# Making the low part of some weight chunks by an accumulating transfer in a hybrid attention layer

## The chip, the cores and the metric

One Trainium2 chip, one of its cores. The metric is device time in microseconds for one execution of the whole layer, as the median of several runs. TensorE is written PE, VectorE DVE, ScalarE ACT, GpSimd POOL, and SyncE, from which most transfers are issued, SP.

## What is computed

One decoder layer on 1024 tokens of width 2048: RMSNorm, one input projection, two groups of heads (a chunked gated delta rule and a chunked causal spatial gate), then one output projection with residual and a final RMSNorm. Only its end matters here:

```python
mix = jnp.concatenate([o_a, o_b], axis=-1) @ w_out[l].astype(x.dtype)
h = h + mix
...
return rms_norm(h, final_norm_w)
```

`w_out` is 2048 x 2048, all in float32.

## The kernel before

Every float32 product is made of three matmuls of a reduced format (float32r). Each operand is split into a high part, the value rounded, and a low part, what the rounding left; the product is high*high + high*low + low*high. `split` (L133) does this: a cast on ACT writes the high part (L135), a subtract on DVE writes the low part from the raw value and the high part (L136).

The output phase (`out_phase`, L850) is a Strassen-like scheme. Left operand and `w_out` are cut into 2 x 2 blocks, and `PRODUCTS` (L809) lists seven block products; for each it names the block or sum of two blocks of the left side, the same of `w_out`, and the blocks of the result to which it is added. In products 0, 2 and 6 (`SUMS`) the sum of two `w_out` blocks has been put into DRAM earlier (`wc_d`); in products 3 and 4 (`SUMB`) it is added on the fly (`wb`, L188); products 1 and 5 use one block as it lies in `w_out`.

Each product runs over two column halves `cb`, and in each over eight chunks k of 128 rows. One chunk is a 128 x 512 piece of the weights, 256 KB: 12 matmuls of 512 columns (L981 high*high, L982 with the low part of the weights, L983 with the low part of the left side) for four row tiles `t`. That is 7 x 2 x 8 = 112 chunks. `prep` (L892) gets a chunk ready: `w_chunk` (L183) loads it into a raw tile `wro` from SP's queue and splits it into `who` and `wlo`; in half 0 `a_prep` does the same for the left operand (`ar`, summed at L885, split into `a`). `run` (L214) prepares chunks three ahead of the one being multiplied. Raw tiles have three buffers (tag `wr`), high and low parts four each (tags `wh`, `wl`), so the cast of a chunk can start only when the fourth chunk before it has been multiplied.

After the last chunk of a half, `evac` (L909) adds the four accumulated tiles into the result blocks `c` on DVE (L919), for a block's first time together with the residual `xres`, loaded through two buffers. `finish` (L925) squares a block that is complete on ACT (`sqh`, L931) and multiplies it by the final norm's weights on POOL (L933), or, for the last quarter of a row tile, computes the row's scale in eleven small steps on DVE (`sth`), scales the four quarters (L951 on DVE, L955 on ACT) and writes them out (L956).

The order on each engine is that of the program after a scheduling layer has placed each instruction; every engine then runs its own list strictly in order. Product 5 is the one in whose first half the rows finished by product 4 are scaled and written out.

Of the kernel before, what the change touches and what calls it, by code (L numbers as in the profile page):

```python
# [8 lines left out]
F32 = mybir.dt.float32  # L9
F32R = mybir.dt.float32r  # L10
I32 = mybir.dt.int32
AF = mybir.ActivationFunctionType
ALU = mybir.AluOpType
# [4 lines left out]
P = 128  # L18
DM = 2048
SEQ = 1024  # L20
T = 512
# [10 lines left out]
def kernel(ctx, tc, x_tok, x_t, w_in, w_v0, w_vb, w_out, conv_w, norm_w, a_log, dt_bias,  # L32
                       hn_w, sgu_w, sgu_b, wsp_t, b_sp, fn_w, out):
    nc = tc.nc
# [98 lines left out]
    def split(hi, lo, src):  # L133

        nc.scalar.copy(hi, src)  # L135
        nc.vector.tensor_tensor(lo, src, hi.bitcast(F32), op=ALU.subtract)  # L136
# [43 lines left out]
        nc.scalar.copy(rb, rp)  # L180
        return rb

    def w_chunk(src, shape, name, keep=None, raw=None, add=None):  # L183
        if raw is None:
            raw = wp.tile(shape, F32, tag="wr", bufs=3, name=f"wr{name}")
        nc.sync.dma_start(raw, src)
        if add:
            nc.vector.tensor_tensor(raw, raw, add[0], op=add[1])  # L188
        hi, lo = keep or (wp.tile(shape, F32R, tag="wh", name=f"wh{name}"), wp.tile(shape, F32R, tag="wl", name=f"wl{name}"))
        split(hi, lo, raw)  # L190
        return hi, lo


# [38 lines left out]
    def w_tile(hf, ct, q):  # L232
        return w_chunk(w_in[ct, :, q * KH:(q + 1) * KH, :], [P, KH, P], f"{hf}_{ct}_{q}")
# [29 lines left out]
    def first_tiles(hf, xs, env, done):  # L263
# [3 lines left out]
        for q in range(KT // 2):  # L267
            def prep(q=q):
                ks = slice(2 * q, 2 * q + 2)
                raw = wp.tile([P, 2, 2, P], F32, tag="wr", bufs=3, name=f"wrf{hf}_{q}")  # L270
                hi = wp.tile([P, 2, 2, P], F32R, tag="wh", name=f"whf{hf}_{q}")
                lo = wp.tile([P, 2, 2, P], F32R, tag="wl", name=f"wlf{hf}_{q}")
                sqs_, sqs[:] = list(sqs), []
                for i in range(2):
                    x, sq = x_load(hf, 2 * q + i)
                    xs.append(x)
                    sqs.append(sq)
                    nc.sync.dma_start(raw[:, i], w_in[(H, 0)[i], :, ks, :])
                    split(hi[:, i], lo[:, i], raw[:, i])
                if q % 3 == 0:  # L280
                    vraw.append(big.tile([P, 3, 2, 288], F32, tag="b8", name=f"v0r{hf}_{q}"))
                v2 = big.tile([P, 2, 2, 288], F32R, tag="b8", name=f"v0{hf}_{q}")[:, :, :, 0:V0]
                vb = w_chunk(w_v0[q], None, None, (v2[:, 0], v2[:, 1]), vraw[-1][:, q % 3, :, 0:V0])
                for sq in sqs_ + (sqs if q == KT // 2 - 1 else []):
                    sq()
                if hf == 0 and q == 5:
                    conv_constants()
                return hi, lo, vb
# [480 lines left out]
    def group_b(hf, xs, st):  # L769
# [3 lines left out]
        for blk in range(1, 4):  # L773
            for k2 in range(KT // 2):
                def mm(w, blk=blk, k2=k2):
                    hi, lo = w
                    if blk == 1 and k2 == 0:
                        sb["rb"] = st["rb"]
                        env["vn"] = st["vn"] + [big.tile([P, NT, T], F32, tag="b8", name=f"vn{hf}_1")]
                    if k2 == 0:  # L780
                        env["acc"] = [proj_bank(f"vb{hf}_{blk}_{i}").rearrange("p (t c) -> p t c", c=256) for i in range(2)]
                    acc, vn = env["acc"], env["vn"]
                    for k in (2 * k2, 2 * k2 + 1):
                        xh, xl = xs[k]
                        for t in range(NT):
                            a, tsl = acc[t // 2][:, t % 2, :], slice(t * P, (t + 1) * P)
                            first, last = k == 0 and t % 2 == 0, k == KT - 1
                            for l, r, fl, sp_ in ((xh, hi, first, False), (xh, lo, False, False), (xl, hi, False, last)):
                                nc.tensor.matmul(a, l[:, tsl], r[:, k % 2, :], start=fl, stop=sp_, skip_group_check=True)  # L789
                        if k % 2 == 0:  # L790
                            tick()
                    if k2 == KT // 2 - 1:
                        for t in range(NT):
                            v = vsl(vn, t, blk * 256, (blk + 1) * 256)
                            nc.scalar.copy(v, acc[t // 2][:, t % 2, :])
                            nc.vector.bn_stats(st["st"][:, t, blk, :], v)
                        if blk == 3:
                            spawn(task_ln(hf, vn, st["st"], sb))
                    tick()
                yield (lambda blk=blk, k2=k2: w_chunk(w_vb[blk - 1, k2], [P, 2, 256], f"vb{hf}_{blk}_{k2}")), mm  # L800
# [26 lines left out]
    def w_quarter(b, cb, k):  # L827

        return w_out[b[1] * 2 + cb, b[0] * HK + k]
# [20 lines left out]
    def out_phase():  # L850
# [29 lines left out]
        def a_prep(n, k):  # L880
            spec = PRODUCTS[n][0]
            src = a_raw(n, spec[0], k)
            if len(spec) > 1:
                dst = src if spec[0] not in KEPT else wk.tile([P, T], F32, tag="cv", bufs=3, name=f"as{n}_{k}")
                nc.vector.tensor_tensor(dst, src, a_raw(n, spec[1], k), op=op[spec[2]])  # L885
                src = dst
            hi, lo = (wk.tile([P, T], F32R, tag=tag, bufs=bufs, name=f"a{i}{n}_{k}")
                      for i, (tag, bufs) in enumerate(ASLOTS[2 * k:2 * k + 2]))
            split(hi, lo, src)
            return hi, lo  # L890

        def prep(n, cb, k):  # L892
            src = w_quarter(PRODUCTS[n][1][0], cb, k) if n not in SUMS else \
                wc_d[SUMS.index(n), cb, k].rearrange("p (o c) -> p o c", o=1)
            keep = None
            if n == LAST and cb == 1 and k < HK - 4:
                keep = [act.tile([P, 1, T], F32R, tag="ah", name=f"wk{i}_{k}") for i in range(2)]
            add = None
            if n in SUMB:
                tag, bufs = SUMB[n]  # L900
                add = wk.tile([P, 1, T], F32, tag=tag, bufs=bufs, name=f"wb{n}_{cb}_{k}")
                nc.sync.dma_start(add, w_quarter(PRODUCTS[n][1][1], cb, k))
                add = add, op[PRODUCTS[n][1][2]]
            w = w_chunk(src, [P, 1, T], f"o{n}_{cb}_{k}", keep, add=add)
            if cb == 0:
                return w, a_prep(n, k)
            return w, None
# [88 lines left out]
        for n in range(LAST + 1):  # L996
            for cb in range(2):
                for k in range(HK):
                    if n == LAST and cb == 1:
                        yield (lambda k=k: prep(LAST, 1, k)), (lambda w, k=k: first_mm(w, k))  # L1000
                    else:
                        yield (lambda n=n, cb=cb, k=k: prep(n, cb, k)), \
                            (lambda w, n=n, cb=cb, k=k: mm(w, n, cb, k, range(NT)))
# [57 lines left out]
```

## Time and profile before

| | us |
|---|---|
| median of 3 runs | 1775.75 |
| lowest and highest | 1774.19, 1779.86 |
| the profiled execution, its own time | 1777.34 |
| its span, first to last instruction | 1775.6 |
| PE busy | 1729.8 (97%) |
| DVE busy | 1265.6 (71%) |
| ACT busy | 736.2 (41%) |
| POOL busy | 261.6 (15%) |
| mean granted TensorE clock | 0.993 |

The profile page gives busy time by engine, the chain of work that ended last, and the costliest groups of instructions by line. A timeline row has start and duration in us, engine, line, output and inputs by the program's names, and in brackets how long the engine had been idle before and who released it. Where an engine waits is read from those brackets; a matmul of 512 columns takes 0.39 us from start to end, but the next one starts 0.23 us after it, since they overlap.

### The profile page before, as it was taken

The numbers are of one execution on the slowest core, as the hardware profiler recorded it, in microseconds if no ns is written. First come the engines' busy times: TensorE is split into PE (matmuls) and PEld (weight loads), VectorE is DVE, ScalarE is ACT, GpSimd is POOL, SyncE is SP. The second block draws the span as 40 slices with busy tenths as digits, with TensorE's granted clock in tenths as the row PEclk, the third lists the DMA queues.
The fourth block names the chain that finished last, engine by engine and source line by source line (L and its number), as shares of the span: only waits on it lengthen the run. The fifth ranks groups of instructions, "written<-read, shape, count | busy, mean of one in ns | idle before, by whom it ended". The sixth has DMA issues, their size and how long they took to land.

```text
span 1775.6 us, 27440 instructions
## 1 busy us (share of the span) xinstructions
PE 1729.8 (97%) x9334; PEld 1456.9 (82%) x9334; DVE 1265.6 (71%) x2985; ACT 736.2 (41%) x1670; POOL 261.6 (15%) x314
## 2 busy tenths in 40 slices
PE   9999999999999999999999999999989999999997
PEld 8778888888997788887887778889878888878876
DVE  7798797987747533758979789794764346777885
ACT  7543534445333222646344443533422233333463
POOL 4120131211201200203012112120030000200121
PEclk9999999999999999999999999999999999999999
DMA  7455445364548734426543535544784457656774
GB/s 240 126 132 139 112 118 151 95 173 133 146 141 259 221 105 127 124 68 172 129 132 89 163 105 151 133 132 116 225 259 115 115 185 235 195 167 188 219 234 148
DMA packets 188893, 275.88 MB, mean 155 GB/s; under 512 B 37936, under 2 KB 70736, under 8 KB 188496
## 3 DMA queue, kind: packets, MB, share of 16 engines
q1 hardware_dynamic: 184064, 261.50, 50.8%
q0 software_dynamic: 4544, 12.62, 2.8%
q8 instruction: 73, 1.20, 0.3%
q14 instruction: 68, 0.56, 0.1%
q10 hardware_dynamic: 144, 0.01, 0.0%
HBM read 224.73 MB, written 49.32 MB: 154 GB/s over the span
## 4 chain that ended last, share of the span: by engine, by line
PE 64%; DVE 16%; DMA 11%; issue 4%; ACT 3%; POOL 1%; SPq 1%; DVEq 0%; ACTq 0%; POOLq 0%
PE acc L239 12%; PE acc L242 12%; PE acc L240 12%; PE vb L789 7%; PE oa L983 3%; PE oa L982 3%; PE oa L981 3%; DVE wl L136 2%; DVE cv L414 2%; DMA ar<-mix_d 2%; DMA xres<-x_tok 2%; DMA ws<-w_out 2%; PE ds L633 1%; PE p L622 1%; DVE fst L567 1%
## 5 line engine op out<-in xcount | busy, mean ns | idle before, releaser
L239 PE MATMUL acc<-xh,wh 128*128 128x512 f32 x1472 | 591.8, 402 | 1.0 <-ACT wh L135 1.0
L242 PE MATMUL acc<-xh,wl 128*128 128x512 f32 x1472 | 577.6, 392 | 5.1 <-DVE wl L136 5.0
L240 PE MATMUL acc<-xl,wh 128*128 128x512 f32 x1472 | 577.1, 392 | 0.0
L135 ACT CAST wh<-wr 128x512 fp32r<-128x512 f32 x368 | 226.1, 618 | 447.2 <-PE acc L240 310.8
L136 DVE TENSOR_TENSOR wl<-wr,wh 128x512 fp32r<-128x512 f32 x368 | 256.7, 700 | 144.2 <-ACT wh L135 139.2
L242 PEld LDWEIGHTS acc<-xh,wl 128*128 128x128 f32 x1472 | 277.6, 189 | 64.9 <-DVE wl L136 6.6
L239 PEld LDWEIGHTS acc<-xh,wh 128*128 128x128 f32 x1472 | 278.1, 189 | 58.0 <-issue 3.0
L240 PEld LDWEIGHTS acc<-xl,wh 128*128 128x128 f32 x1472 | 278.4, 189 | 51.7
L982 PE MATMUL oa<-wlo,a 128*128 128x512 f32 x432 | 168.4, 390 | 2.3 <-DVE wlo L136 2.3
L981 PE MATMUL oa<-who,a 128*128 128x512 f32 x432 | 168.3, 390 | 0.9 <-DVE pczb L405 0.5
L983 PE MATMUL oa<-who,a 128*128 128x512 f32 x432 | 168.2, 389 | 0.7 <-DVE a L136 0.7
L414 DVE SCALAR_TENSOR_TENSOR cv<-pc,cw,cv 128x511 f32<-128x511 f32 (+1 forms) x144 | 110.9, 770 | 8.7 <-ACT cv L411 7.2
L789 PE MATMUL vb<-whvb,xh 128*128 128x256 f32 x384 | 110.5, 288 | 0.0
L789 PE MATMUL vb<-wlvb,xh 128*128 128x256 f32 x384 | 108.6, 283 | 0.0
L789 PE MATMUL vb<-whvb,xl 128*128 128x256 f32 x384 | 108.6, 283 | 0.0
L135 ACT CAST who<-wro 128x512 fp32r<-128x512 f32 x108 | 66.5, 618 | 86.4 <-PE oa L983 41.0
L982 PEld LDWEIGHTS oa<-wlo,a 128*128 128x128 f32 x432 | 81.1, 188 | 20.3 <-DVE wlo L136 3.5
L136 DVE TENSOR_TENSOR wlo<-wro,who 128x512 fp32r<-128x512 f32 x108 | 77.9, 726 | 27.0 <-ACT who L135 26.7
L981 PEld LDWEIGHTS oa<-who,a 128*128 128x128 f32 x432 | 81.1, 188 | 18.4 <-DVE pczb L405 1.0
L983 PEld LDWEIGHTS oa<-who,a 128*128 128x128 f32 x432 | 81.1, 188 | 17.9 <-DVE a L136 1.2
L567 DVE TENSOR_TENSOR fst<-fs 32x31 f32<-32x31 f32 (+15 forms) x248 | 90.4, 365 | 4.2
L569 DVE TENSOR_TENSOR fs<-fs,fst 32x31 f32<-32x31 f32 (+15 forms) x248 | 87.3, 352 | 3.9
(248 smaller groups left out, 2482.1 us busy)
## 6 DMA issues: line engine op xcount, KB each, us to landing
wr<-w_in SPq DMA_DIRECT2D x368, 256.0 KB, 3.3
ws<-w_out SPq DMA_DIRECT2D x64, 256.0 KB, 4.1
wro<-w_out SPq DMA_DIRECT2D x64, 256.0 KB, 3.1
wrvb<-w_vb SPq DMA_DIRECT2D x48, 256.0 KB, 2.7
wc_d<-ws SPq DMA_DIRECT2D x48, 256.0 KB, 3.2
ar<-mix_d SPq DMA_DIRECT2D x48, 256.0 KB, 3.8
wro<-wc_d SPq DMA_DIRECT2D x48, 256.0 KB, 2.7
xr<-x_t SPq DMA_DIRECT2D x32, 256.0 KB, 3.8
```

What stands on the lines that cost most here:

```text
L135: nc.scalar.copy(hi, src)
L136: nc.vector.tensor_tensor(lo, src, hi.bitcast(F32), op=ALU.subtract)
L239: nc.tensor.matmul(acc, hi[:, kk, :], xh, start=(k == 0), stop=False)
L240: nc.tensor.matmul(acc, hi[:, kk, :], xl, start=False, stop=(last and lo is None))
L242: nc.tensor.matmul(acc, lo[:, kk, :], xh, start=False, stop=last)
L414: nc.vector.scalar_tensor_tensor(cv[:, s:], acc[:, :T - s], w, cv[:, s:], op0=ALU.mult, op1=ALU.add)
L567: nc.vector.tensor_tensor(tv, bc(lu[:, k, k + 1:].unsqueeze(2), [32, n, m]), bc(xu[:, k:k + 1, 0:m], [32, n, m]), op=ALU.mult)
L569: nc.vector.tensor_tensor(xu[:, k + 1:, 0:m], xu[:, k + 1:, 0:m], tv, op=ALU.subtract)
L789: nc.tensor.matmul(a, l[:, tsl], r[:, k % 2, :], start=fl, stop=sp_, skip_group_check=True)
L981: nc.tensor.matmul(acc[t], ah[:, tsl], hi[:, 0, :], start=(k == 0), stop=False)
L982: nc.tensor.matmul(acc[t], ah[:, tsl], lo[:, 0, :], start=False, stop=False)
L983: nc.tensor.matmul(acc[t], al[:, tsl], hi[:, 0, :], start=False, stop=(k == HK - 1))
```

## The change

`w_chunk` gets a switch `by_dma`, on for products 1, 2 and 5 and there for every odd k: 3 x 2 x 4 = 24 chunks. In those the DVE subtract is left out. ACT casts the high part as before (new line 192), then writes the negated high part into the low tile (new line 193); a transfer issued from POOL then reads the chunk from DRAM a second time and adds it onto the low tile (new line 194), so that raw minus high part stands there. The raw tile is read by the cast alone.

```diff
-    def w_chunk(src, shape, name, keep=None, raw=None, add=None):
+    def w_chunk(src, shape, name, keep=None, raw=None, add=None, by_dma=False):
         if raw is None:
             raw = wp.tile(shape, F32, tag="wr", bufs=3, name=f"wr{name}")
         nc.sync.dma_start(raw, src)
...
-        split(hi, lo, raw)
+        if by_dma:
+
+            nc.scalar.copy(hi, raw)
+            nc.scalar.activation(lo, hi.bitcast(F32), AF.Copy, scale=-1.0)
+            nc.gpsimd.dma_start(lo, src, accum_op=ALU.add)
+        else:
+            split(hi, lo, raw)
         return hi, lo
...
-            w = w_chunk(src, [P, 1, T], f"o{n}_{cb}_{k}", keep, add=add)
+            w = w_chunk(src, [P, 1, T], f"o{n}_{cb}_{k}", keep, add=add, by_dma=(n in (1, 2, 5) and k % 2 == 1))
```

The lines behind the change stand six lower in the new file. The scheduling layer also places work around the new instructions anew. ACT in the first half of product 5, where `who_0_5` is the high part of chunk 5 of half 0, `sqh` the square of a block and `c` scaled by `sth` the rows that are finished; before:

```order
L931 ACTIVATE sqh_1_2_17023,ssh<-c_1_15508 128x512
L955 ACTIVATE c_0_15507<-c_0_15507,sth 128x512
L955 ACTIVATE c_2_15093<-c_2_15093,sth 128x512
L955 ACTIVATE c_3_15094<-c_3_15094,sth 128x512
L135 CAST who_0_5_17055<-wro_0_5_17053 128x512
L931 ACTIVATE sqh_1_3_17073,ssh<-c_1_15508 128x512
L135 CAST who_0_6_17105<-wro_0_6_17103 128x512
L135 CAST who_0_7_17130<-wro_0_7_17128 128x512
L955 ACTIVATE c_1_15508<-c_1_15508,sth 128x512
```

and now:

```order
L961 ACTIVATE c_3_15094<-c_3_15094,sth 128x512
L192 CAST who_0_5_17073<-wro_0_5_17071 128x512
L937 ACTIVATE sqh_1_3_17092,ssh<-c_1_15513 128x512
L193 ACTIVATE wlo_0_5_17074<-who_0_5_17073 128x512
L135 CAST who_0_6_17124<-wro_0_6_17122 128x512
L135 CAST a_6_17131<-ar_6_17128 128x512
L961 ACTIVATE c_1_15513<-c_1_15513,sth 128x512
L961 ACTIVATE c_4_15095<-c_4_15095,sth 128x512
L961 ACTIVATE c_5_15096<-c_5_15096,sth 128x512
L135 CAST a_7_17157<-ar_7_17154 128x512
L192 CAST who_0_7_17149<-wro_0_7_17147 128x512
```

The negation of chunk 5 stands behind the square, and the cast of chunk 7 has moved behind three scalings and two casts of the left operand; its negation follows after three scalings more.

POOL in products 1 and 2, where `c` times `fw` are the multiplications by the final norm's weights; before, nothing but these stands there:

```order
L967 DMA fw_14923<-fn_w 128x512
L933 TENSOR_TENSOR c_0_15091<-c_0_15091,fw_14921 128x512
L933 TENSOR_TENSOR c_2_15093<-c_2_15093,fw_14921 128x512
L933 TENSOR_TENSOR c_4_15095<-c_4_15095,fw_14921 128x512
L933 TENSOR_TENSOR c_6_15097<-c_6_15097,fw_14921 128x512
```

and now:

```order
L194 DMA wlo_0_7_15434<-w_out 128x512
L194 DMA wlo_1_1_15478<-w_out 128x512
L939 TENSOR_TENSOR c_0_15091<-c_0_15091,fw_14921 128x512
L194 DMA wlo_1_3_15531<-w_out 128x512
L939 TENSOR_TENSOR c_2_15093<-c_2_15093,fw_14921 128x512
L939 TENSOR_TENSOR c_4_15095<-c_4_15095,fw_14921 128x512
L939 TENSOR_TENSOR c_6_15097<-c_6_15097,fw_14921 128x512
L194 DMA wlo_1_5_15586<-w_out 128x512
```

The transfers stand in POOL's list between the multiplications, which wait for squares on ACT.

PE at chunk 7 of product 5's first half, before high*high, high*low and low*high of a row tile in turn:

```order
L981 MATMUL oa_0_0_16962<-who_0_7_17130,a_7_17137 128x512
L982 MATMUL oa_0_0_16962<-wlo_0_7_17131,a_7_17137 128x512
L983 MATMUL oa_0_0_16962<-who_0_7_17130,a_7_17138 128x512
L981 MATMUL oa_0_1_16963<-who_0_7_17130,a_7_17137 128x512
L982 MATMUL oa_0_1_16963<-wlo_0_7_17131,a_7_17137 128x512
```

and now:

```order
L987 MATMUL oa_0_0_16980<-who_0_7_17149,a_7_17157 128x512
L987 MATMUL oa_0_1_16981<-who_0_7_17149,a_7_17157 128x512
L988 MATMUL oa_0_0_16980<-wlo_0_7_17150,a_7_17157 128x512
L989 MATMUL oa_0_0_16980<-who_0_7_17149,a_7_17158 128x512
L988 MATMUL oa_0_1_16981<-wlo_0_7_17150,a_7_17157 128x512
```

One matmul that doesn't need the low part has moved ahead of the first that does; in the first chunks of the second half three have.

## Rows read from the trace of the kernel before

**Rows 1.** The page's chain that ended last: shares of the span by engine.

```profile
PE 64%; DVE 16%; DMA 11%; issue 4%; ACT 3%; POOL 1%; SPq 1%; DVEq 0%; ACTq 0%; POOLq 0%
```

**Rows 2.** Products 1, 2, 3, 5 as stretches: length, busy by engine, clock, DMA share, GB/s.

```profile
1499.90:1544.10 44.20, 43.83 (x194) 35.97 (x193) 32.64 (x49) 16.22 (x32) 6.00 (x4) 1.00 0.71 213
1544.10:1589.80 45.70, 43.76 (x193) 35.93 (x192) 37.15 (x54) 17.26 (x34) 5.95 (x4) 1.00 0.55 155
1589.80:1633.30 43.50, 43.50 (x193) 36.03 (x192) 32.72 (x53) 14.13 (x24) 0.00 (x0) 1.00 0.67 207
...
1676.90:1722.30 45.40, 44.32 (x194) 35.78 (x193) 39.07 (x92) 27.86 (x54) 5.33 (x4) 1.00 0.76 253
```

**Rows 3.** Timeline: chunks 1/0/7 and 1/1/7 (cast, first low matmul), low matmul of 2/0/4.

```profile
1515.19 0.62 ACT L135 CAST who<-wro 128x512 fp32r<-128x512 f32 x1 [4.96 <-DMA wro<-w_out]
...
1519.68 0.50 PE L982 MATMUL oa<-wlo,a 128*128 128x512 f32 x1 [0.37 <-DVE wlo L136]
...
1538.77 0.62 ACT L135 CAST who<-wro 128x512 fp32r<-128x512 f32 x1
...
1541.57 0.39 PE L982 MATMUL oa<-wlo,a 128*128 128x512 f32 x1
...
1557.28 0.50 PE L982 MATMUL oa<-wlo,a 128*128 128x512 f32 x1 [1.95 <-DVE wlo L136]
```

**Rows 4.** Timeline: cast of chunk 2/1/3 and its first low matmul.

```profile
1568.27 0.62 ACT L135 CAST who<-wro 128x512 fp32r<-128x512 f32 x1 [2.10 <-PE oa L983]
...
1576.45 0.39 PE L982 MATMUL oa<-wlo,a 128*128 128x512 f32 x1
```

**Rows 5.** Groups by line: count, busy us, mean ns, idle before; subtract and POOL's multiplication.

```profile
L136 DVE TENSOR_TENSOR wlo<-wro,who 128x512 fp32r<-128x512 f32 x108 | 77.9, 726 | 27.0 <-ACT who L135 26.7
...
L933 POOL TENSOR_TENSOR c<-c,fw 128x512 f32<-128x512 f32 x24 | 34.5, 1455 | 258.3 <-ACT sqh L931 258.3
```

**Rows 6.** Transfers from POOL's queue, issue start to landing: 256 KB (L434), 512 KB (`em`).

```profile
L434 POOL DMA_DIRECT2D ut<-swapo x16: 558/567/589, 252.1 to 1329.4; - x16
...
DMA to landing us min/median/max: 3.0/3.9/5.6
...
em<-gcd POOLq DMA_DIRECT2D x4, 512.0 KB, 5.9
```

**Rows 7.** Timeline of product 5, half 0: cast of chunk 5 and what follows.

```profile
1689.26 0.61 ACT L135 CAST who<-wro 128x512 fp32r<-128x512 f32 x1
...
1690.39 1.12 ACT L135 CAST who<-wro 128x512 fp32r<-128x512 f32 x2
1692.09 1.95 ACT L955 ACTIVATE c<-c,sth 128x512 f32<-128x512 f32 x3 [0.57 <-DVE sth L946]
...
1690.73 0.50 PE L982 MATMUL oa<-wlo,a 128*128 128x512 f32 x1
```

**Rows 8.** Microseconds of product 5, first and last of four: columns as in rows 2.

```profile
1688.00:1689.00 1.00, 1.00 (x6) 0.84 (x5) 1.00 (x5) 1.00 (x3) 0.00 (x0) 1.00 1.03 393
...
1691.00:1692.00 1.00, 1.00 (x5) 0.78 (x5) 1.00 (x7) 0.51 (x1) 0.00 (x0) 1.00 1.10 381
```

**Rows 9.** PE after two gaps: timeline rows, and microseconds (length, PE, clock, DMA).

```profile
1307.62 2.05 PE L650 MATMUL at<-ut,gae 128*128 128x128 f32 x8 [4.96 <-DVE s L747]
...
1307.00:1308.00 1.00, 0.38 (x2) 0.58 0.90 344
1308.00:1309.00 1.00, 1.00 (x6) 0.50 0.62 244
1309.00:1310.00 1.00, 1.00 (x6) 0.50 0.75 166
1310.00:1311.00 1.00, 1.00 (x5) 0.72 0.60 207
...
828.31 0.50 PE L242 MATMUL acc<-xh,wl 128*128 128x512 f32 x1 [2.85 <-DVE wl L136]
...
830.00:831.00 1.00, 1.00 (x4) 0.50 0.75 111
```

## The prediction, made before the changed kernel ran

> **What bounds the kernel now.** I read the chain of work first, then the seven output products as stretches, then who waited for whom on TensorE, then the timeline around each wait. A chunk is named by product, half (`cb`) and k, so 1/0/7 is product 1, half 0, k 7; the casts of a w_out chunk stand in the trace in program order, 112 of them, and a chunk needs 12 matmuls. The chain spends 64% of the span on PE [rows 1]. In the output phase that share is higher still: a product whose data is always there takes 43.5 us with PE busy throughout (product 3). Products 1, 2 and 5, the three that are changed, take 44.2, 45.7 and 45.4 us [rows 2]. What they have above product 3 is 0.7 + 2.2 + 1.9 = 4.8 us, and that is all that can be won here. Two of those waits, 2.3 us together, are PE waiting for a low part that VectorE makes, 0.37 at 1519.68 and 1.95 at 1557.28 [rows 3].
>
> So VectorE is late at places, and taking 24 of its subtracts away is aimed at that. But it is a question of latency, not of busy time. A low part must be ready when the second matmul of its chunk starts. The reader should see the lead, from the start of a chunk's cast on ScalarE to that matmul. Where nothing is late it is 8.18 us, since the cast starts at the moment PE gives back the buffer of the fourth chunk before (four buffers each for high and low parts) and three chunks lie between: cast of 2/1/3 at 1568.27, use at 1576.45 [rows 4]. In the 24 changed chunks it runs from 8.18 down to 1.47 us.
>
> **The change part by part.** Removed: 24 subtracts of 0.726 us on VectorE [rows 5], 17.4 us of busy time, none of it on PE. Their cover is the matmuls; only where VectorE is late does PE gain.
>
> Added on ScalarE: 24 activations that write the negated high part. The nearest row is the cast of the same 128x512, 0.62 us [rows 3], so 24 x 0.62 = 14.9 us on an engine with 16 to 28 us of work in a 45 us stretch [rows 2]. It has room, but the activation stands in its order behind other work.
>
> Added on GpSimd's queue and the DMA engines: 24 accumulating transfers of 256 KB. No row shows one. A plain transfer of 256 KB from that queue lands 3.0 to 5.6 us after its issue starts, 3.9 in the middle; one of 512 KB takes 5.9 [rows 6]. An accumulating one has to read the destination besides the source, so 512 KB are read. The lower bound is 3.0, the plain transfer at its best; a gain is excluded, since it does no less. The upper bound is two plain ones in series, 7.8. I take 5.9, the row that moves as many bytes. The raw load stays, so the chunk is read from DRAM twice.
> The Trainium skill ("DMA: Bandwidth & Descriptors", section on the anatomy of a SWDGE DMA) gives 2.0 us plus bytes over 436 GB/s for a transfer issued by GpSimd, an estimate of 2.6 us for 256 KB; the rows here lie above it, and with it the chain below would take 3.84 us.
>
> The new chain of a changed chunk is cast 0.62, negation 0.62, transfer 5.9 = 7.15 us with nothing in between. The old one was 0.62 + 0.73 = 1.35 us where VectorE was free. Against 8.18 us of lead that is hidden; of the 24 chunks four have a lead of 7.15 us or more (7.88 to 8.18 us). A missing lead does not add up over chunks: one wait of PE moves all later uses back by as much, so what counts is the worst chunk of each run of late ones.
>
> Product 1. Chunk 1/0/7 is cast at 1515.19, because its raw load came late; it was used at 1519.68, after a wait of 0.37, so without it at 1519.31 [rows 3]. One changed subtract ahead of it (1/0/3) is gone, so the cast comes perhaps 0.7 earlier: 1514.5 + 7.15 = 1521.65, a wait of 2.3 in place of 0.37: **+1.9 us**. The shortest lead after it is 1/1/7, cast 1538.77, used 1541.57, 2.80 us [rows 3]. PE is then 2.3 later and the four subtracts between (1/0/7, 1/1/1, 1/1/3, 1/1/5) are gone, 2.8: 7.9 us, enough. On GpSimd's queue the transfers of 1/1/3 and 1/1/5 stand behind one and three multiplications of finished rows, which wait for squares on ScalarE. I cost that at nothing, since the leads of both grow by PE's 2.3 us; if that cover is gone, a multiplication is 1.46 us [rows 5].
>
> Product 2. PE waited 1.95 us for the unchanged low part 2/0/4, at the end of that same jam of VectorE [rows 3]. With PE later and VectorE lighter it goes: **-1.95 us**.
>
> Product 5. The cast of 5/0/5 starts at 1689.26, held up by a square and six scalings that wait for VectorE, and its first low matmul is at 1690.73, a lead of 1.47 us [rows 7]. Two subtracts fewer bring the cast 1.4 forward, the negation of 5/0/3 puts ScalarE 0.6 back: 1688.46. The new order sets a square between the cast and the negation; from cast to the next instruction behind such a square the trace has 1690.39 - 1689.26 = 1.13 us [rows 7]. So the negation runs 1689.6 to 1690.2 and the transfer lands at 1696.1, a wait of 5.4 us. For 5/0/7 two blocks of three scalings (1.95 us each in the trace) and four casts at 0.52 spacing [rows 7] stand before the negation: it ends at 1696.8, lands at 1702.7. PE, with its new order, needs it at 1696.4 + 5.4 = 1701.8: 0.9 more. The 1.9 us that product 5 lost before are absorbed in this. 5.4 + 0.9 - 1.9 = **+4.4 us**.
> In these microseconds the DMA engines are full: mean busy share 1.03 to 1.10 from 1688 to 1692, the finished rows being written out [rows 8], so a transfer here hardly beats its middle value. The Trainium skill says why another queue brings no relief ("DMA: Bandwidth & Descriptors", "Issuing engines are not separate DMA queues"): all queues run on the same 16 engines and interleave. Its rule gives no number of its own.
>
> The clock. After a gap of 4.96 us on PE the granted clock stood at 0.58, 0.50, 0.50 and 0.72 in the next four microseconds, i.e. at 1.2 of 2.4 GHz: 1.7 us lost. After the gap of 2.85 us at 828 the same level was granted; after the one of 1.95 us no fall shows in the rows of its stretch, product 2, where the clock reads 1.00 [rows 2, 9]. So the 5.4 us wait costs **+1.7 us** besides, and the 2.3 us one, between the two, half: **+0.9 us**.
>
> Sum: 1.9 - 1.95 + 4.4 + 1.7 + 0.9 = +6.95 us. The profiled execution took 1777.34 us, 1.6 above the median 1775.75, so the sum gives 1784.3 on it and **1782.7 us** on the median. With transfers of 3.9 to 7.0 us this case spans 1778 to 1789.
>
> **The rivals.**
> Hidden, no measurable change: the accumulating transfer costs what a plain one does, 3.9 us. Then 1/0/7 is ready at 1519.65, a wait as before (0); product 2 gives 1.95 back; 5/0/5 waits 1694.1 - 1690.7 = 3.4, 5/0/7 0.9 more, less 1.9: +2.4; the clock +1.7. Sum +2.2: 1778. For it: all plain rows. Against it: the destination has to be read too. The fit of the Trainium skill ("DMA: Bandwidth & Descriptors", the same section) would put it here as well.
>
> Not slower: VectorE's relief is larger than I take it, since its waits for residual loads and its collisions with GpSimd's multiplications shrink together with its queue, and the late casts come 3 us or more earlier. It decides at 5/0/5: the lead there has to grow from 1.47 to some 5.2 us. Then all 4.8 us come back: 1771. More is not to be had, as PE is busy in all the rest. Against it: that cast waits for scalings which hang on eleven small steps of VectorE that are not removed.
>
> Much slower: the accumulating transfer is a read of both, then a write, 7.8 us or more. Then the chain takes 9.05 us and exceeds the 8.18 us lead even where nothing is late, and the ring of four buffers becomes the limit: each round of four chunks is longer by 0.87 us. Products 1 and 2 have eight rounds, 7.0 us; product 5 has 7.3 + 0.9 - 1.9 and two free rounds of 0.87, 8.0; product 2's 1.95 goes; two clock falls 3.4. Sum +16.5: 1792. At 11.7 us, three in series, it is 4.8 us a round, over 57 us.
>
> **How the numbers follow.** Forecast 0.42, hidden 0.32, not slower 0.08, much slower 0.18. About 0.3%, 5.3 us, is what a measurement of this kernel can tell from no change. Of the forecast 0.08 lie under +5.3, of the not-slower case 0.03 over -5.3 (its 4.8 plus scatter). Same: 0.32 + 0.08 + 0.05 = 0.45; faster 0.03; slower 0.34 + 0.18 = 0.52. The range goes from 1773, which leaves out the best of the not-slower case, to 1802, which leaves out half of the much-slower one.
>
> **What would show it.** Right: PE waits for `wlo` that end with a DMA, the longest in product 5's first half, then 1 or 2 us in product 1; product 2 near 43.5 us; transfers on GpSimd's queue landing in 5 to 7 us. A landing near 4 us is the hidden case; over 8 us, with a wait in each group of four chunks, the ring. Wrong altogether: PE waits in products 1, 2 and 5 for something else, or a cast of 5/0/5 more than 3 us earlier.

## The result and the profile after

The changed kernel takes 1800.68 us (median of 4 runs), the kernel before 1777.45 in the same comparison: ratio 1.0114, 95% interval 1.0094 to 1.0134, that is 20.3 us slower (16.7 to 23.8). The sign was the likelier one in the prediction, and the time lies just inside its range; the value named, 1782.7, is 18 us too low.

In the profile after, the lines behind the change stand six lower: L987 is high*high, L988 the matmul with the low part of the weights, L989 the one with the low part of the left side. The profiled execution took 1795.5 us, the lowest of the four. Its chain of work, beside [rows 1]: PE's share fell from 64% to 58%, that of DVE rose from 16% to 18%, and that of the DMA from 11% to 13%.

```profile
PE 58%; DVE 18%; DMA 13%; issue 5%; ACT 4%; POOL 1%; SPq 1%; DVEq 0%; ACTq 0%; POOLq 0%
```

Products 1, 2, 3 and 5 of the changed kernel as stretches, columns as in [rows 2] (length, PE, weight loads, DVE, ACT, POOL, clock, DMA share, GB/s):

```profile
1497.10:1549.80 52.70, 46.35 (x194) 36.85 (x193) 29.17 (x44) 21.80 (x42) 13.05 (x13) 0.97 0.86 234
1549.80:1595.00 45.20, 44.16 (x194) 35.89 (x193) 30.64 (x43) 20.89 (x40) 11.30 (x11) 1.00 0.76 185
1595.00:1638.50 43.50, 43.50 (x193) 36.02 (x192) 32.87 (x53) 14.13 (x25) 0.00 (x0) 1.00 0.67 204
...
1682.00:1740.45 58.45, 48.71 (x194) 37.81 (x193) 40.14 (x89) 31.23 (x62) 11.66 (x11) 0.94 0.84 237
```

Product 1 went from 44.20 to 52.70 (+8.5), product 2 from 45.70 to 45.20 (-0.5), product 5 from 45.40 to 58.45 (+13.05); product 3 is unchanged. That is +21 us. The two profiled spans differ by 18.2 us (1793.8 against 1775.6), since in this execution everything in front of product 1 took 2.8 us less. Each length splits into PE's idle time (length less PE busy) and PE's busy time, which grows when the clock is low. Idle: product 1 from 0.4 to 6.35, product 5 from 1.1 to 9.7, together 14.6 more. Busy: product 1 +2.5, product 5 +4.4, together 6.9. VectorE's busy time fell as meant, 32.64 to 29.17 in product 1, and bought nothing.

Who PE waited for in the output phase of the changed kernel (total us, times, longest):

```profile
PE oa L988 <- DMA wlo<-w_out: 15.4, 9, 3.9
PE oa L988 <- DMA wlo<-wc_d: 1.0, 2, 0.7
PE oa L988 <- DVE wlo L136: 0.7, 1, 0.7
```

The two waits for VectorE's low part, 2.3 us [rows 3], are replaced by eleven for a transfer, 16.4 us. Four of them with their chain, in a timeline of the changed kernel (chunks 1/0/1, 1/1/7, 5/0/5, 5/1/1 in turn; start, us, engine):

```profile
1495.04 0.61 ACT L192 CAST who<-wro 128x512 fp32r<-128x512 f32 x1
1495.69 0.63 ACT L193 ACTIVATE wlo<-who 128x512 fp32r<-128x512 f32 x1
1496.63 0.92 POOL L194 DMA_DIRECT2D wlo<-w_out  x1 [39.25 <-ACT wlo L193]
1503.29 0.66 PE L988 MATMUL oa<-wlo,a 128*128 128x512 f32 x1 [3.09 <-DMA wlo<-w_out]
...
1540.49 0.62 ACT L192 CAST who<-wro 128x512 fp32r<-128x512 f32 x1
...
1547.14 0.50 PE L988 MATMUL oa<-wlo,a 128*128 128x512 f32 x1 [1.76 <-DMA wlo<-w_out]
...
1692.63 0.60 ACT L192 CAST who<-wro 128x512 fp32r<-128x512 f32 x1
1693.14 0.63 ACT L937 ACTIVATE sqh<-c 128x512 f32<-128x512 f32 x1
...
1693.76 0.62 ACT L193 ACTIVATE wlo<-who 128x512 fp32r<-128x512 f32 x1
...
1694.68 0.87 POOL L194 DMA_DIRECT2D wlo<-w_out  x1 [7.39 <-ACT wlo L193]
1701.06 0.50 PE L988 MATMUL oa<-wlo,a 128*128 128x512 f32 x1 [3.87 <-DMA wlo<-w_out]
...
1711.52 0.60 ACT L192 CAST who<-wro 128x512 fp32r<-128x512 f32 x1
...
1718.01 0.50 PE L988 MATMUL oa<-wlo,a 128*128 128x512 f32 x1 [1.40 <-DMA wlo<-w_out]
```

From cast to waiting matmul these are 8.25, 6.65, 8.43 and 6.49 us: cast and negation 0.62 us each (at 5/0/5 with a square between them), about 0.3 us until GpSimd starts the issue, the rest the transfer. The sum had 7.15, in the middle of these. The length of the chain was about right; how often it would be paid was not.

### The profile page after: what moved, and what is told of

It reads as the page before. It is cut to its first block, busy times and chain, and to the rows that moved or that the text cites. A ratio compares the mean times of both kernels' runs of the same rounds, so it can differ in the third digit from the quotient of the medians.

```text
span 1793.8 us, 27489 instructions
## 1 busy us (share of the span) xinstructions
PE 1735.4 (97%) x9334; PEld 1457.2 (81%) x9334; DVE 1256.0 (70%) x2961; ACT 749.2 (42%) x1694; POOL 283.4 (16%) x338
## 4 chain that ended last, share of the span: by engine, by line
PE 58%; DVE 18%; DMA 13%; issue 5%; ACT 4%; POOL 1%; SPq 1%; DVEq 0%; ACTq 0%; POOLq 0%
PE acc L245 10%; PE acc L248 10%; PE acc L246 10%; PE vb L795 7%; PE oa L988 4%; PE oa L989 4%; PE oa L987 4%; DVE wl L136 3%; DVE cv L420 2%; DVE fs L575 2%; DMA ws<-w_out 2%; DVE fst L573 2%; DMA wr<-w_in 1%; DMA pc<-swapk 1%; DMA xres<-x_tok 1%
## 5 line engine op out<-in xcount | busy, mean ns | idle before, releaser
L988 PE MATMUL oa<-wlo,a 128*128 128x512 f32 x432 | 171.6, 397 | 17.1 <-DMA wlo<-w_out 15.4
L989 PE MATMUL oa<-who,a 128*128 128x512 f32 x432 | 170.2, 394 | 0.0
L987 PE MATMUL oa<-who,a 128*128 128x512 f32 x432 | 168.8, 393 | 0.0
L988 PEld LDWEIGHTS oa<-wlo,a 128*128 128x128 f32 x432 | 82.2, 190 | 39.6 <-DMA wlo<-w_out 19.5
L987 PEld LDWEIGHTS oa<-who,a 128*128 128x128 f32 x432 | 82.3, 190 | 17.7 <-DVE pczb L411 0.4
L989 PEld LDWEIGHTS oa<-who,a 128*128 128x128 f32 x432 | 82.2, 190 | 16.9
L136 DVE TENSOR_TENSOR wlo<-wro,who 128x512 fp32r<-128x512 f32 x84 | 63.1, 753 | 31.0 <-ACT who L135 30.8
L135 ACT CAST who<-wro 128x512 fp32r<-128x512 f32 x84 | 51.9, 618 | 73.7 <-PE oa L989 42.8
```

The costliest lines, as they stand in the source:

```text
L987: nc.tensor.matmul(acc[t], ah[:, tsl], hi[:, 0, :], start=(k == 0), stop=False)
L988: nc.tensor.matmul(acc[t], ah[:, tsl], lo[:, 0, :], start=False, stop=False)
L989: nc.tensor.matmul(acc[t], al[:, tsl], hi[:, 0, :], start=False, stop=(k == HK - 1))
```

## The experiments

Differences in microseconds below are the ratio's distance from 1 times the time of the kernel before in the same comparison, the interval in brackets. Lengths of products are those of one profiled execution each.

**One product at a time.** The switch is on for product 1, 2 or 5 alone.

```
by_dma=(n == 1 and k % 2 == 1)     # or n == 2, or n == 5
```

> The transfer replaces the subtract in product 1 alone (8 chunks). The theory read from the trace after: product 1 took 52.7 us there against 44.2 before, so this kernel is about 8.5 us slower than before, near 1786. My sum on record gave product 1 a wait of 1.9 us more and 0.9 for the clock, so near 1780. If the loss came from product 5 alone or from something that the three share, it is within 2 us of before.

> The transfer replaces the subtract in product 2 alone (8 chunks). My sum on record: 1.95 us faster, 1775.5. The trace after: product 2 took 45.2 us against 45.7, so between 1 us faster and 1 us slower. If a chunk by transfer costs about the same wherever it is (21 us over 24 chunks), it is 7 us slower, near 1784.

> The transfer replaces the subtract in product 5 alone (8 chunks). The trace after: product 5 took 58.4 us against 45.4, so 13 us slower, near 1790; my sum on record gave 6.1, near 1783.5. If the products do not add up, because a late product 1 changes what comes later, the three kernels together do not give the 21 us of the change.

Measured: product 1 alone +5.3 us [2.1, 8.4], product 2 alone +0.9 [-1.8, 3.6], product 5 alone +11.7 [7.5, 16.0]. Together that is 17.9, against 20.3 [16.7, 23.8] for all three: the three parts add up within their intervals. Products 1 and 5 as stretches, each in the kernel in which it alone is changed; first product 1:

```profile
1497.98:1551.04 53.06, 47.32 (x194) 38.16 (x192) 29.03 (x44) 21.26 (x41) 11.75 (x12) 0.94 0.85 225
```

Product 5:

```profile
1679.26:1736.93 57.67, 48.11 (x193) 37.60 (x192) 39.85 (x89) 31.26 (x61) 11.67 (x11) 0.94 0.83 241
```

These are the lengths of the full change, 52.70 and 58.45, within 1 us. Where product 1 is 8.9 us longer, product 2 behind it is back at 43.52 and has lost its 2.2 us; that is why the time rises by less than product 1 does. Alone, product 2's transfers lengthen it from 45.70 to 48.15 with waits of 3.7 us in all, the longest 1.4.

**The transfer left out, and a transfer that only writes.** In the first kernel the low part stays at the negated high part; in the second the transfer overwrites it with the raw chunk instead of adding.

```
-            nc.gpsimd.dma_start(lo, src, accum_op=ALU.add)
+            nc.gpsimd.dma_start(lo, src)        # second kernel; first: no transfer
```

> Left out: the accumulating transfer, so that the low part of the 24 chunks is the negated high part. Subtracts gone and negations on ScalarE as in the change. Latency theory: the chain is cast and negation, 1.25 us, no wait of the matmul engine for a low part remains, and up to the 4.8 us that products 1, 2 and 5 had over product 3 come back: 1773 to 1776. Rival, the extra work on ScalarE and the new order cost the time: still 10 us or more slower than before.

> The 24 transfers write the chunk into the low tile instead of adding it (so the low part is the whole chunk); all else as in the change, the negation before it included. If it is the adding that costs, the landing falls from 5.2 us to the 3.9 us of other transfers of that queue, each of the eleven waits shrinks by about 1.3 us and the kernel is 8 to 12 us slower than before, near 1787. If the cost is any transfer in that place, landing and time stay as in the change, near 1799.

Without the transfer the time is that of before, +0.7 us [-2.3, 3.6]: the 24 subtracts that VectorE no longer does, the negations and the new order are together worth nothing net, and the gain that was expected did not come. Product 2 gains 1.4 us (44.37), but product 5 loses 3.5:

```profile
1675.49:1724.43 48.94, 45.75 (x194) 37.04 (x192) 38.14 (x90) 31.40 (x62) 5.19 (x4) 0.97 0.74 240
```

So product 5 can lose time without any transfer. What is left to cause it is the negations and the new order of work around them, which is taken up below.

With a plain transfer in the same place it is +11.8 us [7.8, 15.7]. Some 12 of the 20 us are thus the price of any transfer there, some 8, give or take 5, that of adding. The profiled executions put the adding lower: products 0 to 5 together rose by 16.7 us with the plain transfer and by 20.4 with the adding one, 4 us apart. How long the two kinds take from the start of the issue to landing, in the kernel with plain transfers:

```profile
L194 POOL DMA_DIRECT2D wlo<-w_out x16: 528/531/587, 1499.0 to 1729.8; - x16
...
DMA to landing us min/median/max: 2.9/4.1/6.7
```

and in the changed kernel:

```profile
L194 POOL DMA_DIRECT2D wlo<-w_out x16: 866/874/919, 1496.6 to 1731.7; - x16
...
DMA to landing us min/median/max: 4.1/5.2/6.9
```

Adding costs 1.1 us of landing at the median. The Trainium skill ("DMA: Bandwidth & Descriptors", the anatomy of a SWDGE DMA) would give an estimate of 2.6 us for 256 KB from GpSimd; the fastest plain one here, 2.9, is near that, the median of 4.1 is not.

**The subtract on GpSimd.** The 24 low parts are computed by GpSimd from raw and high part, without a transfer.

```
-            nc.scalar.activation(lo, hi.bitcast(F32), AF.Copy, scale=-1.0)
-            nc.gpsimd.dma_start(lo, src, accum_op=ALU.add)
+            nc.gpsimd.tensor_tensor(lo, raw, hi.bitcast(F32), op=ALU.subtract)
```

> In the same 24 chunks the subtract is done by GpSimd, from the raw tile and the high part, with no negation and no transfer. Latency theory: the chain is cast 0.62 and about 1.45 us on GpSimd, 2.1 us, shorter than nearly every lead, and VectorE has its relief: 0 to 4 us faster than before, 1773 to 1777. Rival, anything taken off VectorE and put into GpSimd's queue behind its multiplications comes too late: 5 us or more slower.

Measured +5.7 us [2.7, 8.7]; the expected gain did not come. GpSimd's part is quick against the transfer, 1.30 us at the median:

```profile
L193 POOL TENSOR_TENSOR wlo<-wro,who x24: 1273/1300/1791, 1499.6 to 1722.8; 128x512 fp32r<-128x512 f32 x24
```

and PE waits 0.3 us for it in all. What PE waits for instead is VectorE's own low parts (4.9 us, the longest 3.6) and a cast (3.4). In this kernel VectorE's subtracts of the left side took 868 ns in the mean, 752 before, both in products 1 to 5. The Trainium skill ("SBUF — State Buffer", SBUF: two separate sides) says that VectorE and GpSimd share a pair of ports, which the one that starts first holds for a whole instruction while the other blocks; the longer subtracts fit that. The same subtracts took 783 ns in the kernel before with a deeper ring (next experiment), where GpSimd does none, so not all of the rise need be GpSimd's. Whether the longer subtracts are all of the 5.7 us, no run here tells, since the order of the work changed too.

**A deeper ring.** High and low parts get five buffers instead of four and are prepared four chunks ahead; the room comes from two other tiles. Once on the kernel before, once on the changed one.

```
-    def run(chunks, ahead=3):
+    def run(chunks, ahead=4):
...
-        hi, lo = keep or (wp.tile(..., tag="wh", ...), wp.tile(..., tag="wl", ...))
+        hi, lo = keep or (wp.tile(..., tag="wh", bufs=5, ...), wp.tile(..., tag="wl", bufs=5, ...))
...
-        gl = wk.tile([P, NT, 64], F32, tag="gl", bufs=3, ...)
+        gl = wk.tile([P, NT, 64], F32, tag="gl", bufs=2, ...)
-        tmp = wk.tile([32, 256], F32, tag="fst", bufs=1, ...)
+        tmp = wk.tile([32, 256], F32, tag="ys", bufs=1, ...)
```

> The kernel before with five buffers instead of four for high and low parts and chunks prepared four ahead instead of three (room is made by one buffer less of a tile of the delta rule and by two of its tiles sharing one). A control for the next one. Expected within 4 us of before, as the waits there are few.

> The change with the same five buffers and four chunks ahead. If the four buffers set the lead, it grows by one chunk, 2.72 us, from 8.2 to 10.9, all waits below 2.7 us vanish and the long ones shrink to about 1: 2 to 6 us slower than the kernel with five buffers without the change. If late raw loads and VectorE's jams set the lead, it stays 12 us or more slower than that one.

The kernel before with the deeper ring takes 1773.77 us, ratio 0.9961 [0.9944, 0.9977], 6.9 us [4.1, 10.0] faster than before, more than the 4 us that had been allowed for: it beats both kernels. PE has no wait in its output phase; products 1, 2 and 5 as stretches:

```profile
1497.64:1541.16 43.52, 43.52 (x193) 36.04 (x192) 31.80 (x47) 15.78 (x31) 5.99 (x4) 1.00 0.71 218
1541.16:1584.91 43.75, 43.75 (x194) 35.96 (x192) 38.52 (x57) 17.82 (x35) 5.98 (x4) 1.00 0.58 169
...
1671.95:1715.47 43.52, 43.52 (x194) 36.04 (x192) 38.75 (x91) 27.33 (x53) 5.69 (x4) 1.00 0.78 257
```

Of the 4.8 us that the prediction called winnable in products 1, 2 and 5, a chunk more of lead wins 4.5: products 0 to 5 together take 261.4 us instead of 266.8, which is 5.4 of the 6.8 us by which the profiled span is shorter (1768.8 against 1775.6).

The changed kernel gains nothing by the same edit: ratio 1.0092 [1.0072, 1.0111], 16.4 us above the kernel before and some 23 above its own base with five buffers. Its longest wait, at chunk 5/1/1, shows what held the work there; SP, ACT and PE:

```profile
1706.77 6.06 SPq L962 DMA_DIRECT2D out<-c  x8
1712.89 1.85 SPq L186 DMA_DIRECT2D wro<-w_out  x3
...
1717.57 0.62 ACT L192 CAST who<-wro 128x512 fp32r<-128x512 f32 x1 [4.47 <-DMA wro<-w_out]
...
1725.53 0.79 PE L988 MATMUL oa<-wlo,a 128*128 128x512 f32 x1 [6.09 <-DMA wlo<-w_out]
```

The fifth buffer was free 12.8 us before that cast. The cast waited for its raw load, and the load stood on SP's queue behind eight stores of finished rows. The same kernel's casts of 1/0/7 and 1/1/1 also waited for their raw loads, 6.63 and 5.96 us. The lead at such a chunk is set by when its raw load is issued, not by the number of buffers.

**Half a product at a time, and another product.** The first two split product 1, the third takes the second half of product 5, the fourth puts the eight transfers into product 0, where the low part is otherwise made by VectorE.

```
by_dma=(n == 1 and cb == 0 and k % 2 == 1)     # or n == 1 and cb == 1; or n == 5 and cb == 1
by_dma=(n == 0 and k % 2 == 1)                 # the fourth
```

> Transfers in the first half of product 1 alone (4 chunks). Theory A, jams move with TensorE: after a wait the evacuation, the residual loads and the casts move back along with TensorE, so each half pays its own waits. Then this kernel has the wait of about 3.1 us at 1/0/1 and one fall of the clock (1.7 us), product 1 is 44.2 + 3.1 + 1.7 - 0.4 = about 48.5 us, no DMA wait in its second half, and the time is 3 to 5 us above the kernel before; together with the next kernel the rise of product 1 adds up to that of both halves (53.06 - 44.2 = 8.9). Theory B, mine at first, one worst chunk counts: the wait of 3.1 lets the second half catch up, and the second half adds only what its own wait exceeds this one: the rise of both halves is that of the dearer half alone, so one of the two kernels must show +8 or more.

> Transfers in the second half of product 1 alone (4 chunks). The trace of before has leads of 6.2, 3.8, 3.5 and 2.8 us there, the chain takes about 6.5 us. Theory A: one wait of 2.5 to 3.5 us by 1/1/3 and a smaller one or two behind it, with one fall of the clock product 1 is 48 to 49.5 us, the time 2 to 5 us above before (product 2 gives up to 2 back); the rise of this kernel and of the first half alone add up to about 8.9. Theory B: either this or the first half alone shows +8 or more in product 1, and the other is contained in it.

> Transfers in the second half of product 5 alone (4 chunks). In the trace of before their leads are 5.2, 4.4, 5.9 and 6.8 us. Theory A, each half pays for itself: waits of 1.5 to 2.5 us at 5/1/1 or 5/1/3, product 5 at 48 to 50 us (before 45.4), the time 2 to 4 us above before. Rival: the second half's waits in the changed kernel came only from its first half, whose finished rows were written late so that the raw loads of 5/1/0 to 5/1/3 started 10 us later: then product 5 stays within 1 us of 45.4 and the time does not move.

> Transfers for every odd chunk of product 0 alone (8 chunks, one third of the change). Here no finished rows are written, no residual is loaded by the middle of the product, and the leads are 6 to 8.2 us. If the place decides (leads, jams), waits are at most 1 us in all, product 0 stays within 1 us of 44.35 us, and the time moves by less than 2 us. If the transfers themselves cost (8 x about 0.8 us as in the change, 20.3 / 24), product 0 grows by 6 to 7 us wherever they stand.

Product 1 with its first half changed, as a stretch:

```profile
1501.17:1550.96 49.79, 46.03 (x193) 36.97 (x192) 31.78 (x46) 18.65 (x36) 9.13 (x8) 0.97 0.75 219
```

its longest wait, at 1/0/1, from the timeline:

```profile
1507.14 0.56 PE L988 MATMUL oa<-wlo,a 128*128 128x512 f32 x1 [2.86 <-DMA wlo<-w_out]
```

With its second half changed, the stretch:

```profile
1501.08:1550.53 49.45, 44.80 (x194) 35.76 (x192) 30.74 (x48) 19.70 (x39) 9.19 (x8) 1.00 0.78 222
```

and its longest wait, at 1/1/3:

```profile
1536.18 0.50 PE L988 MATMUL oa<-wlo,a 128*128 128x512 f32 x1 [2.78 <-DMA wlo<-w_out]
```

The first half alone lengthens product 1 by 5.6 us and the time by 3.7 [0.5, 7.1], the second half alone by 5.3 and 3.4 [1.1, 5.7]. Both together lengthened it by 8.9. If the worst chunk alone counted, the rise of both would be that of the dearer half, and one of the two would have shown it; neither does, and theory B falls. Theory A had the two adding up to 8.9; they add up to 10.8, so a part of the second half's waits is indeed covered by the first half's, but a small one. Theory A also wanted one fall of the clock in each; there is one in the first (after the gap of 2.86) and none in the second.

The second half of product 5 alone, the stretch:

```profile
1674.97:1723.26 48.29, 44.38 (x193) 35.83 (x192) 37.29 (x89) 30.07 (x58) 9.12 (x8) 1.00 0.83 258
```

and its longest wait for a transfer:

```profile
1704.32 0.50 PE L988 MATMUL oa<-wlo,a 128*128 128x512 f32 x1 [2.82 <-DMA wlo<-w_out]
```

Product 5 is 2.9 us longer, with one wait of 2.82 at 5/1/1, as theory A said; the rival, that the second half's waits come from the first half alone, falls. The time, +5.7 us [2.8, 8.4], where 2 to 4 had been expected, is above what the stretch explains; the profiled execution was the fastest of its ten, so this excess has no place in a trace.

Product 0 is the miss. It took +7.8 us [5.2, 10.5], and product 0 itself grew from 44.35 to 49.20 (from its first matmul to that of product 1), though its leads were long. Its stretch:

```profile
1456.00:1505.50 49.50, 45.61 (x195) 35.78 (x193) 18.54 (x31) 18.64 (x32) 7.23 (x9) 1.00 0.93 270
```

the cast of chunk 0/0/7, in the timeline:

```profile
1472.24 0.62 ACT L192 CAST who<-wro 128x512 fp32r<-128x512 f32 x1 [5.74 <-DMA wro<-wc_d]
```

and the landing of its eight transfers:

```profile
DMA to landing us min/median/max: 4.2/6.4/8.5
```

The DMA share of the stretch is 0.93 (0.74 in the same stretch of the kernel before). The transfers land in 6.4 us at the median instead of 5.2, and the raw loads come later too: ACT stood 5.74 us before the cast above until its load was there. PE's waits for transfers there are 2.9 us in five pieces, the longest 0.9. From cast to waiting matmul these five chunks took 7.27 to 10.11 us, about the 8.19 that the ring of four buffers allows. That is near the limit that the much-slower rival described; no run changes the ring here. Products 1 and 2 behind it are 1.0 and 1.9 us longer as well (45.2 and 47.6). In product 2 the wait at 2/0/4 for VectorE's low part is 2.17 us instead of 1.95, and this time the clock fell behind it (0.59, 0.50, 0.50 and 0.70 in four microseconds, 1.7 us lost). The expectation that the place alone decides was wrong: eight more transfers of 256 KB in a stretch whose DMA engines are that busy cost 4.9 us in that stretch, although the leads are longest there. Which part of it is the longer landing and which the later raw loads, the run doesn't tell apart.

## Why the prediction was right or wrong

**The bound and the sign: right.** Latency decided, not VectorE's busy time. The waits end with a transfer; the longest stands at 5/0/5; the wait at 2/0/4 for VectorE is gone. The kernel without the transfer shows no net gain from VectorE's relief, with the negations and the new order in it.

**The range: luck.** The forecast's own case, transfers of 3.9 to 7.0 us, ended at 1789. The transfers landed in 4.1 to 6.9 us, inside that case, and the time is 1800.68. It lies in the range only because the range reaches to 1802 for half of the much-slower rival, whose mechanism products 1, 2 and 5 don't show.

**The chain of 7.15 us: about right.** The landing assumed at 5.9, from the row of 512 KB [rows 6], measured 5.2 at the median and 6.9 at most. The bound of 7.8, two plain ones in series, was not reached here, and the much-slower rival with it: its ring did not become the limit. From 1/0/5 to 1/1/1 of the changed kernel the casts start as soon as a buffer comes free, with a lead of 8.19 us, and PE does not wait. Its 1792 is nearer to the time than the forecast, but by a mechanism that this trace doesn't show. What was costed at nothing, the transfers' place behind multiplications on GpSimd's queue, was worth next to nothing: the transfers of 1/1/3 and 1/1/5 started 0.3 us after their negations.

**The step that failed: "a missing lead does not add up over chunks".** The step took it that one wait of PE moves all later uses back while the casts stay where they are. They don't stay, and the lead that a wait gives is soon lost again. One reason is the ring. Behind the wait at 1/0/1 the uses of 1/0/2 to 1/0/4 came 10.88 to 12.41 us after their casts; but from 1/0/5 to 1/1/1 each cast waited until PE gave a buffer back, and the lead is 8.19 at each of them. The cast of 1/1/1 in the changed kernel:

```profile
1518.57 0.62 ACT L192 CAST who<-wro 128x512 fp32r<-128x512 f32 x1 [2.10 <-PE oa L989]
```

The other is the end of a half. There VectorE adds the accumulated tiles into the result, which waits for PE's last matmul; behind it on VectorE, ACT and SP's queue stand low parts, casts and raw loads, and they move back with PE. That is read from the order of the rows; which link holds which chunk, no run isolates. How far the casts move is measured, from the first matmul of the product. It is seen best in the kernel with the first half of product 1 alone changed, whose second half is made as before. Cast and first low matmul of 1/1/7:

```profile
1543.69 0.62 ACT L135 CAST who<-wro 128x512 fp32r<-128x512 f32 x1
...
1548.47 0.39 PE L988 MATMUL oa<-wlo,a 128*128 128x512 f32 x1
```

Beside [rows 3] the use comes 5.6 us later into the product and the cast 3.6 later: of 5.6 us only 2.0 became lead (2.80 to 4.78). In the changed kernel itself product 1 starts at 1497.1, before at 1499.9. The use of 1/1/7 is, without its own wait, 48.3 us into the product instead of 41.7, 6.6 later; its cast is at 43.4 instead of 38.9, 4.5 later. So the lead grew from 2.80 to 4.89 only, and PE waits again. 5/1/1 stands thus in the timeline of the kernel before (cast and first low matmul):

```profile
1698.32 0.60 ACT L135 CAST who<-wro 128x512 fp32r<-128x512 f32 x1
...
1703.48 0.39 PE L982 MATMUL oa<-wlo,a 128*128 128x512 f32 x1
```

Product 5 starts there at 1676.9, and at 1682.0 in the changed kernel. Its use came 8.0 us later without its own wait, and its cast 8.0 later as well: a lead of 5.16 before and, without the wait, 5.09 after. The waits in front had bought nothing. Instead of one wait of 2.3 us in product 1 there are four, 3.09, 0.51, 0.99 and 1.76; instead of two in product 5 there are five for transfers and one for VectorE. The half-by-half runs bear it out: the rises of the two halves of product 1 nearly add up.

**Product 1, its first chunk.** I costed 1/0/7, the worst one, and passed over 1/0/1, whose lead was 5.17 us (cast at 1497.66, use at 1502.83 in the trace of before). It is the first changed chunk of the product, so nothing had moved PE before it, and it waits 3.09. Behind it, 1/0/7 had its full lead back and did not wait. A first chunk should be costed first, whichever is worst.

**Product 5, the order.** The prediction saw casts, squares and scalings change places on ACT, and costed the negations behind them. It did not cost the queue behind those scalings: the stores of finished rows wait for them, and on SP's queue the raw load of 5/1/0 stands behind the stores. The changed kernel, SP and ACT:

```profile
1696.06 6.32 SPq L962 DMA_DIRECT2D out<-c  x8
1702.43 1.99 SPq L186 DMA_DIRECT2D wro<-w_out  x3
...
1699.17 0.62 ACT L192 CAST who<-wro 128x512 fp32r<-128x512 f32 x1 [1.40 <-DMA wro<-w_out]
1699.70 1.94 ACT L961 ACTIVATE c<-c,sth 128x512 f32<-128x512 f32 x3
```

and the kernel before, SP:

```profile
1685.69 5.31 SPq L956 DMA_DIRECT2D out<-c  x8
1691.10 1.90 SPq L186 DMA_DIRECT2D wro<-w_out  x2
```

That load is issued 20.4 us into product 5 instead of 14.2, after eight stores of which the last wait for scalings that now stand behind the cast of 5/0/7. In the kernel without the transfer it is just as late (1696.08, 20.6 us into its product 5), and there product 5 is 3.5 us longer; 1.7 of these are a fall of the clock behind a wait of 2.11 us for a cast. In the changed kernel product 5's six waits are 0.68, 3.87 (at 5/0/5, 5.4 in the prediction), 0.75 (at 5/0/7, 0.9 in the prediction), 0.73, 1.40 and 2.31 us, 9.7 in all against 1.1 before, and the clock fell behind two of them. How much of the 13 us is the order and how much the transfers, the runs don't separate: alone, the order with the negations costs 3.5 and the second half's transfers 2.9, and a wait in one place hides part of the others.

**The clock.** The sum had 2.6 us for it. The granted clock fell to half three times, after the waits of 3.09, 3.87 and 2.31 us. The microseconds after the second (length, PE, ..., clock, DMA share, GB/s):

```profile
1701.00:1702.00 1.00, 0.94 (x3) 0.80 (x4) 0.00 (x0) 1.00 (x3) 0.00 (x0) 0.72 1.00 381
1702.00:1703.00 1.00, 1.00 (x3) 0.78 (x3) 0.00 (x0) 0.16 (x1) 0.55 (x1) 0.50 1.04 399
1703.00:1704.00 1.00, 1.00 (x4) 0.74 (x3) 0.00 (x0) 0.00 (x0) 0.32 (x1) 0.50 1.05 385
1704.00:1705.00 1.00, 1.00 (x4) 0.80 (x3) 0.00 (x0) 0.00 (x0) 0.00 (x0) 0.58 0.96 260
```

Level and time are those of [rows 9], 1.7 us lost each. The size per fall was right, the number of falls was not: about 5 us instead of 2.6. The rest of the 6.9 us of busy time is not the clock. Each wait makes PE's busy time some 0.3 us longer besides, an estimate from the kernel with the second half of product 1 changed: three waits for transfers, clock 1.00, and busy 44.80 instead of 43.83.

**The sum again.** Product 1 was given +2.8 with its clock and is +8.5; product 2 was given -1.95 and is -0.5, since two short waits for transfers (1.0 us) stand where the long one went; product 5 was given +6.1 with its clock and is +13.05.

## What to carry to other kernels

A wait at one place gives the work behind it little more lead when that work is fed by the stage that waited: cost each stretch between two such couplings (here each half) by itself and add the waits up, as a bound from above (10.8 us for the 8.9 of product 1). A transfer in place of a short instruction needs its latency in lead at every chunk, the first one included, and its order is costed through the queues: the loads behind the stores behind the instruction that moved. Where engines wait only for work that starts too late, one buffer more and one step further ahead can be worth more than taking work off an engine.

## What the runs showed of the hardware

An accumulating transfer of 256 KB from GpSimd landed in 5.2 us at the median (4.1 to 6.9), a plain one in the same place in 4.1 (2.9 to 6.7); in product 0, with the DMA share at 0.93, the accumulating one took 6.4 (4.2 to 8.5). Its issue held GpSimd for 0.87 us, that of the plain one for 0.53.

The length of a gap on PE did not tell by itself whether the clock falls. After gaps of 2.31, 2.86, 3.09 and 3.87 us the granted clock went to 0.50, and after one of 2.17 with product 0 alone changed; after gaps of 2.78 and 2.82 us, in the kernels with the second half of product 1 and of product 5 alone, and after one of 2.88 in product 1 with plain transfers, the clock of the whole stretch reads 1.00.
